# Taking attention pieces a margin later in PE's planned order, a larger gate share, and merge loads behind the sums

## The chip, the cores and the metric

The kernel runs on one core of one Trainium2 chip, in one launch. The metric is the device time of that core in microseconds; lower is better. All data are 32-bit floats. TensorE is PE in what follows, VectorE is DVE, ScalarE is ACT, GpSimd is POOL, and SP is the queue from which most DMAs are issued.

## What is computed

A backbone of two layers over 512 latent tokens and 256 context tokens of width 1024. Each layer normalises its rows, runs four kinds of attention (A, B, C, D, each with four heads of 64), merges them through sigmoid gates, and ends in a mixture of 32 experts. What the change touches is the attention and the merge:

```python
def merge_branches(h, outs, w_gate, b_gate, w_branch, w_out):
    y = None
    for n in range(N_BRANCH):                       # four branches
        t = jax.nn.sigmoid(h @ w_gate[n] + b_gate[n]) * (outs[n] @ w_branch[n])
        y = t if y is None else y + t
    return y @ w_out

for l in range(DEPTH):                              # DEPTH = 2
    h, hc = modulate(x, ...), modulate(ctx, ...)    # [512, 1024], [256, 1024]
    y, yc = token_mixer(h, hc, ..., with_ctx=l < DEPTH - 1)   # w_in, attention A B C D, merge_branches
    x = x + gt1 * y                                 # and ctx likewise in layer 0
    x = x + gt2 * hier_moe(modulate(x, ...), ...)   # top-1 group, top-2 expert in it
```

Layer 0 runs over all 768 tokens, layer 1 over the 512 latent ones (its context only serves as keys). `h @ w_gate[n]` and `outs[n] @ w_branch[n]` are the two products whose order the change moves.

## The kernel before, in words

**Products.** A product of two float matrices is made of three matmuls: each operand is split into a rounded high part and the rest (names end in H and L), and high x high, high x low and low x high are summed in PSUM (line 251). Weights come from DRAM as `wraw`, ACT makes wH (L275), DVE or, where it is told so, POOL makes wL (L276).

**Order on PE.** `dense` runs norm, attention, gates and merge of a layer with PE's order written by a planner, class `Flow`. It holds items (a piece of work with those it depends on, a latency after them, slots of SBUF that it takes, and resources that it needs: "S" for one of two score buffers in PSUM called `sps`, "bk" for one of four PSUM banks called `bk`, "P" for one of three buffers of probabilities) and a clock of its own, made of assumed durations (the tables LT). `run` goes round: the **fill**, which is `gates()`, is taken when it can go and when its work so far is below `ratio` times the work of everything else (FILL: 0.8 in layer 0, 0.4 in layer 1); otherwise `pick` takes the first item of a window of 80 that is ready and whose resources are free by the planner's clock; if there is none, the fill again. The orders of DVE, ACT, POOL and SP are made afterwards by the scheduler of the language, from the same program; each of these queues runs its instructions in that fixed order.

**Attention.** For a pair of query blocks `scores` puts q x k into an `sps` (`sps<-sk,sq`, `sps<-sc,sq`), DVE takes a minimum (L1132), ACT the exponential into `P` (L1152), DVE scales it (L1157), PE transposes `P` in groups of three 128 x 128 blocks into a `bk` (`bk<-ident,P`, L256), ACT copies each group into `pt` (L1169), and `values` multiplies with V (`bk<-pt,V`); the result goes to DRAM (`o`). Projections of later halves stand between these pieces.

**Gates.** Thirty-two units a layer, unit (n, m) for branch n and 128 output columns m, n in ORDER = (1, 0, 2, 3): 24 matmuls 128x512 (`bk<-hT,wH`, `bk<-hT,wL`; in layer 0 also 24 of 128x256 for the context), tanh on ACT (L1199), and a store to DRAM (`thd<-th`). In layer 0 ten segments of the modulation weights (`mod_seg`) are part of the fill; a step of one has to wait for the DMA of the step before.

**Merge.** `load(n)` brings back the attention's results of branch n (`orw`, in layer 0 also `orc`), splits them into oHL and ocHL, and loads and splits the weights w_br (two `wraw`). `unit(n, m)` then loads the gate from DRAM into `thm`, a buffer of the same three as `P`, makes 6 matmuls 128x512 (`sps<-oHL,wH`, `sps<-oHL,wL`; in layer 0 another 6 of 128x256), multiplies gate and product on DVE (L1253 for the first n, L1249 for the others) and adds into the sums `yl` on DVE and `yc` on POOL (L1255). For the last n the finished sums are split into yH and yL. A unit depends on `ys` (the item that allocates the sums, which itself depends on the end of the whole attention), on its load and on its gate. `w_out(0)` loads four tiles of the output weights; POOL makes their wL.

Of the kernel before, what the change touches and what calls it, by code (L numbers as in the profile page):

```python
# [142 lines left out]
class Flow:  # L143
# [13 lines left out]
    def use(self, cls, after):  # L157
        self.used.append((cls, after))

    def can(self, need):  # L160
        for c in need:
            if c == "norms" and not all(it.done for it in self.norms):
                return False
            if c in self.busy and min(self.busy[c]) > self.clk:
                return False
            if c == "pt2" and self.left["pt1"] < 2 or c == "pt1" and self.left["pt1"] < 1:
                return False
            if c in ("P", "dup") and self.left[c] < 1:
                return False
        return True  # L170
# [13 lines left out]
        self.used = []  # L184
        return self.clk - t0

    def pick(self, todo):
        blocked, soon = False, []
        for it in todo[:WINDOW]:
            if it.on:  # L190
                ready = it.ready
            else:
                if any(not d.done for d in it.deps):
                    continue
                ready = max([d.t + it.lat for d in it.deps], default=0.0)
                if it.slots and (blocked or it.slots > self.free):
                    blocked = True
                    continue
            if ready > self.clk:
                soon.append(ready)  # L200
            elif self.can(it.need):
                return it, soon
        return None, soon

    def run(self, first=()):

        todo = [it for it in self.items if not it.done]
        while todo:
            if first and all(it.done for it in first):
                return  # L210
            f = self.fill
            ok = f is not None and not f.done and f.ready <= self.clk and all(d.done for d in f.deps) and self.can(f.need)
            if ok and self.filled < self.ratio * self.main:
                self.filled += self.step(f)
                continue
            it, soon = self.pick(todo)
            if it is not None:
                self.main += self.step(it)
                if it.done:
                    todo.remove(it)  # L220
                continue
            if ok:
                self.filled += self.step(f)
                continue
            if f is not None and not f.done:
                soon.append(f.ready)
            soon += [t for b in self.busy.values() for t in b]
            soon = [t for t in soon if t > self.clk]
            assert soon, "nothing can go on"
            self.clk = min(soon)  # L230


class Build:
# [971 lines left out]
    def merge(self):  # L1205
        nc, l, f = self.nc, self.l, self.fl
# [64 lines left out]
        ys = f.item(self.nop(0, sums), deps=self.ends, slots=4 + 2 * self.wc)  # L1271
# [2 lines left out]
        self.ysplit, self.wo = ([], []), {}  # L1274
        for n in ORDER:
            if n == ORDER[-1]:
                f.items.append(f.item(self.nop(0, lambda: self.w_out(0)), deps=self.ends[-1:], slots=9))
            e = {1: 1, 0: 3, 2: 5, 3: 7}[n]
            ld = f.item(self.nop(0, lambda n=n: load(n)), deps=[self.ends[e], self.gate[8 * n]], lat=0.0, slots=k)
            us = [f.item(unit(n, m), deps=[ys, ld, self.gate[8 * n + m]], lat=self.LT["th"], need=("S",)) for m in range(8)]  # L1280
            f.items += [ld] + us + [f.item(self.nop(6 + self.wc), deps=us)]

# [699 lines left out]
NT2 = 3  # L1982
GE = False
UPOOL = (3,)
FILL = (0.8, 0.4)
WINDOW = 80
ORDER = (1, 0, 2, 3)
PEX = 2
# [27 lines left out]
```

## Time and profile before

| | us |
|---|---|
| median of 3 runs | 2233.44 (2230.81 to 2235.84) |
| the profiled execution: its own time | 2233.74 |
| its span in the trace | 2232.0 |
| layer 0: attention's first and last matmul | 45.5, 713.6 |
| layer 0: first and last merge matmul | 723.0, 839.5 |
| layer 0: first expert matmul | 971.1 |
| layer 1: first transpose of h, last attention matmul | 1297.4, 1771.4 |
| layer 1: first and last merge matmul | 1777.3, 1870.0 |
| layer 1: first expert matmul, end | 1956.1, 2232.0 |

The lower rows are starts in the trace, from the start of the span. A "tail" is the stretch from the attention's last matmul to the merge's last: 713 to 841 and 1771 to 1870. In each stretch PE's busy time against the length says how much PE stood idle; the waits say for whom. Durations of matmuls are read from the distance between the starts of neighbours in a row, since the printed length of one includes its way through the pipeline.

### The profile page before, as it was taken

The numbers are of one execution on the slowest core, as the hardware profiler recorded it, in microseconds if no ns is written. First come the engines' busy times: TensorE is split into PE (matmuls) and PEld (weight loads), VectorE is DVE, ScalarE is ACT, GpSimd is POOL, SyncE is SP. The second block draws the span as 40 slices with busy tenths as digits, with TensorE's granted clock in tenths as the row PEclk, the third lists the DMA queues.
The fourth block names the chain that finished last, engine by engine and source line by source line (L and its number), as shares of the span: only waits on it lengthen the run. The fifth ranks groups of instructions, "written<-read, shape, count | busy, mean of one in ns | idle before, by whom it ended". The sixth has DMA issues, their size and how long they took to land. (4 is left out here: it accounts for less than half of the span.)

```text
span 2232.0 us, 34108 instructions
## 1 busy us (share of the span) xinstructions
PE 2068.5 (93%) x13005; PEld 1524.7 (68%) x13005; DVE 1288.5 (58%) x2655; ACT 808.8 (36%) x1817; POOL 295.7 (13%) x321
## 2 busy tenths in 40 slices
PE   5999999999999988969999979999999998699997
PEld 3878777777887877934444468877888787644443
DVE  4464454345544565677777766555466476746655
ACT  4454454344444221212222235565455432211112
POOL 1101100011100144230000031000020013200000
PEclk8999999999999998979999989999999999899999
DMA  7452443543223555679999423112212387699992
GB/s 280 144 195 95 152 155 113 171 149 119 81 78 115 188 187 197 227 254 402 365 366 364 178 76 107 55 48 90 90 46 86 121 259 263 226 379 407 406 406 80
DMA packets 141813, 430.92 MB, mean 193 GB/s; under 512 B 19344, under 2 KB 32032, under 8 KB 141648
## 3 DMA queue, kind: packets, MB, share of 16 engines
q1 hardware_dynamic: 127120, 388.36, 48.4%
q0 software_dynamic: 13088, 35.10, 4.8%
q10 hardware_dynamic: 1440, 5.24, 0.6%
q8 instruction: 104, 1.70, 0.3%
q14 instruction: 61, 0.50, 0.1%
HBM read 398.67 MB, written 36.78 MB: 195 GB/s over the span
## 5 line engine op out<-in xcount | busy, mean ns | idle before, releaser
L251 PE MATMUL bk<-hT,wH 128*128 128x512 f32 (+1 forms) x1760 | 480.2, 360 | 2.8 <-ACT wH L275 2.1
L251 PEld LDWEIGHTS bk<-hT,wH 128*128 128x128 f32 x1760 | 300.1, 189 | 51.4 <-issue 8.1
L251 PE MATMUL bk<-hT,wL 128*128 128x512 f32 (+1 forms) x880 | 311.8, 354 | 7.6 <-DVE wL L276 7.6
L1786 DVE TENSOR_TENSOR x<-x,sps 128x1024 f32<-128x1024 f32 x166 | 195.5, 1216 | 101.0 <-PE sps L1785 100.6
L1727 PE MATMUL bk<-e,xT 128*64 128x512 f32 x1056 | 245.8, 603 | 0.0
L251 PE MATMUL bk<-wH,hT 128*128 128x256 f32 x1248 | 240.5, 287 | 1.3 <-DVE sk L276 1.0
L251 PEld LDWEIGHTS bk<-wH,hT 128*128 128x128 f32 x1248 | 200.0, 193 | 5.3 <-DVE sk L276 1.3
L251 PEld LDWEIGHTS bk<-hT,wL 128*128 128x128 f32 x880 | 166.3, 189 | 33.4 <-DVE wL L276 9.8
L275 ACT ACTIVATE wH<-wraw 128x1024 fp32r<-128x1024 f32 x132 | 139.1, 1058 | 125.1 <-DMA wraw<-in_w_gate_dram 41.5
L276 DVE TENSOR_TENSOR wL<-wraw,wH 128x1024 fp32r<-128x1024 f32 x112 | 138.8, 1245 | 70.2 <-ACT wH L275 39.4
L251 PE MATMUL bk<-wL,hT 128*128 128x256 f32 x624 | 177.2, 284 | 0.0
L1727 PEld LDWEIGHTS bk<-e,xT 128*64 128x64 f32 x1056 | 72.1, 138 | 142.9 <-issue 125.7
L1152 ACT ACTIVATE P<-sps,m 128x768 f32<-128x768 f32 (+2 forms) x160 | 126.5, 792 | 77.0 <-DVE m L1132 52.7
L1169 ACT ACTIVATE pt<-bk 128x384 f32<-128x384 f32 (+1 forms) x288 | 120.8, 467 | 74.7 <-PE bk L256 73.6
L1785 PE MATMUL sps<-yeH,to 128*128 128x512 f32 x332 | 142.7, 430 | 2.4 <-ACT yeH L275 1.4
L256 PE MATMUL bk<-ident,P 128*128 128x128 f32 x800 | 121.2, 282 | 19.2 <-ACT pt L1169 7.3
L1785 PE MATMUL sps<-yeL,to 128*128 128x512 f32 x332 | 132.2, 398 | 1.7 <-DVE yeL L276 1.7
L322 POOL TENSOR_TENSOR rr<-rs,mhalf 128x1 f32<-128x1 f32 (+1 forms) x72 | 52.3, 727 | 572.5 <-DVE rs L318 500.9
L1750 PE MATMUL bk<-e,gT 128*64 128x512 f32 x528 | 122.3, 606 | 1.5 <-ACT gT L1743 1.5
L256 PEld LDWEIGHTS bk<-ident,P 128*128 128x128 f32 x800 | 91.7, 142 | 46.7 <-ACT pt L1169 15.4
L251 PEld LDWEIGHTS bk<-wL,hT 128*128 128x128 f32 x624 | 120.3, 193 | 0.6
L1733 ACT ACTIVATE eth<-bk 128x256 f32<-128x256 f32 x33 | 12.7, 385 | 285.7 <-PE bk L1727 285.7
(355 smaller groups left out, 3671.4 us busy)
## 6 DMA issues: line engine op xcount, KB each, us to landing
e<-in_w_dram SPq DMA_DIRECT2D x384, 512.0 KB, 7.5
wmod<-in_w_mod_dram SPq DMA_DIRECT2D x96, 512.0 KB, 4.6
wraw<-in_w_gate_dram SPq DMA_DIRECT2D x64, 512.0 KB, 4.0
wraw<-in_w_in_dram SPq DMA_DIRECT2D x36, 512.0 KB, 4.9
thd<-th SPq DMA_DIRECT2D x64, 256.0 KB, 3.4
thm<-thd SPq DMA_DIRECT2D x32, 384.0 KB, 3.1
wraw<-in_w_br_dram SPq DMA_DIRECT2D x16, 512.0 KB, 4.0
wraw<-in_w_out_dram SPq DMA_DIRECT2D x16, 512.0 KB, 6.1
```

The source lines that it names most:

```text
L251: return self.nc.tensor.matmul(out, lhsT, rhs, **kw)
L256: return self.nc.tensor.transpose(out, src, self.ident if ident is None else ident)
L275: nc.scalar.activation(H, src, AF.Copy)
L276: (eng or nc.vector).tensor_tensor(L, src, H.bitcast(F32), op=ALU.subtract)
L322: self.nc.gpsimd.tensor_tensor(r[:, :n], o[:, :n], self.mhalf.to_broadcast([128, n]), op=ALU.pow)
L1152: nc.scalar.activation(Pt[:, :n], S[:, lo:768], AF.Exp, scale=-1.0, bias=m, accum_out=sm)
L1169: nc.scalar.activation(PT[gi][:, :w, qi * 128:(qi + 1) * 128], v, AF.Copy)
L1727: nc.tensor.matmul(box["h"][64 * z:64 * z + 64, :], xT(k, z), W(z, k // 2)[:, (k % 2) * 512:(k % 2 + 1) * 512], start=k == 0, stop=k == 7, ...
L1733: nc.scalar.activation(th[s], H[s, :256], AF.Tanh, scale=0.5)
L1750: nc.tensor.matmul(Y[n][64 * z:64 * z + 64, :], gT[:, k, 64 * z:64 * z + 64], W(z, 4 + k)[:, n * 512:(n + 1) * 512], start=k == 0, stop=k ...
L1785: nc.tensor.matmul(ps[:, c], to[s, t * 128:(t + 1) * 128], w[s, c], start=i == 0, stop=i == 1)
L1786: nc.vector.tensor_tensor(self.x1[t] if out is None else out, self.x1[t], ps, op=ALU.add)
```

## The change

`can` and `pick` get a margin: while the fill could go (`ok`), an item counts as ready, and a PSUM buffer as free, only when it has been so for MARGIN = 1000 units of the planner's clock. When the fill can't go, the margin is 0. The ratio of the fill goes from (0.8, 0.4) to (0.85, 0.45). In `merge()`, `w_out(0)` and `load(n)` of all branches but the first wait for `ys`, so that the sums get their slots first, and the first load may start only if slots for itself and for the sums are left. PE's instructions are the same in number and kind.

```diff
-    def can(self, need):
+    def can(self, need, margin=0.0):
...
-            if c in self.busy and min(self.busy[c]) > self.clk:
+            if c in self.busy and min(self.busy[c]) + margin > self.clk:
                 return False
...
-    def pick(self, todo):
+    def pick(self, todo, margin):
...
-            if ready > self.clk:
+            if ready + margin > self.clk:
                 soon.append(ready)
-            elif self.can(it.need):
+            elif self.can(it.need, margin):
                 return it, soon
...
-            it, soon = self.pick(todo)
+            it, soon = self.pick(todo, MARGIN if ok else 0.0)
...
             if n == ORDER[-1]:
-                f.items.append(f.item(self.nop(0, lambda: self.w_out(0)), deps=self.ends[-1:], slots=9))
+                f.items.append(f.item(self.nop(0, lambda: self.w_out(0)), deps=[ys], slots=9))
             e = {1: 1, 0: 3, 2: 5, 3: 7}[n]
-            ld = f.item(self.nop(0, lambda n=n: load(n)), deps=[self.ends[e], self.gate[8 * n]], lat=0.0, slots=k)
+            early = n == ORDER[0]
+            ld = f.item(self.nop(0, lambda n=n: load(n)), deps=[self.ends[e], self.gate[8 * n]] + ([] if early else [ys]),
+                        lat=0.0, slots=k + early * ys.slots)
...
-FILL = (0.8, 0.4)
+FILL = (0.85, 0.45)
+MARGIN = 1000.0
```

What that does to the order is seen at three places. The first is PE near the end of layer 1's attention (branch D). `ident,P` are the transposes of probabilities, `sk,sq` and `sc,sq` scores, `pt,V` values, `hT,wH` and `hT,wL` gates. Before:

```order
L251 MATMUL bk<-hT,wL 128x512
L256 MATMUL bk<-ident,P 128x128 x12
L251 MATMUL sps<-sk,sq 128x512 x2
L251 MATMUL sps<-sc,sq 128x256 x2
L251 MATMUL sps<-sk,sq 128x512 x2
L251 MATMUL sps<-sc,sq 128x256 x2
L251 MATMUL bk<-hT,wH 128x512 x2
L251 MATMUL bk<-hT,wL 128x512
L251 MATMUL bk<-pt,V 64x256 x12
```

and now:

```order
L251 MATMUL bk<-pt,V 64x256 x12
L256 MATMUL bk<-ident,P 128x128 x3
L251 MATMUL sps<-sk,sq 128x512 x2
L251 MATMUL sps<-sc,sq 128x256 x2
L251 MATMUL bk<-hT,wH 128x512 x2
L251 MATMUL bk<-hT,wL 128x512
L256 MATMUL bk<-ident,P 128x128 x6
L251 MATMUL sps<-sk,sq 128x512 x2
L251 MATMUL sps<-sc,sq 128x256 x2
L251 MATMUL bk<-hT,wH 128x512 x2
L251 MATMUL bk<-hT,wL 128x512
L256 MATMUL bk<-ident,P 128x128 x3
```

Twelve transposes, four PSUM banks' worth, stood in one piece; now the groups stand apart, with gates and scores between them.

The second place is DVE at the first merge load of layer 0, `load(1)`: oHL and ocHL are its splits, of `orw` and `orc`, and the wL with neighbours wraw, wH are splits of weights, in both orders of a gate and of w_br. The L1132, L1156 and L1157 rows belong to scores. Before:

```order
L276 TENSOR_TENSOR oHL_7406<-orw_7402,oHL_7405 128x1024
L1132 TENSOR_REDUCE m_7444<-sps_7439 128x1
L1132 TENSOR_REDUCE m_7457<-sps_7452 128x1
L1156 RECIPROCAL rc_7449<-sum_7447 128x1
L1157 TENSOR_SCALAR P_7446<-P_7446,rc_7449 128x768
L276 TENSOR_TENSOR ocHL_7412<-orc_7409,ocHL_7412 128x512
L276 TENSOR_TENSOR wL_7418<-wraw_7415,wH_7417 128x1024
L1156 RECIPROCAL rc_7462<-sum_7460 128x1
L276 TENSOR_TENSOR wL_7502<-wraw_7499,wH_7501 128x1024
```

and now:

```order
L919 TENSOR_TENSOR dup_7458<-xnh_7449,g3_5853 128x3x64
L276 TENSOR_TENSOR oHL_8084<-orw_8080,oHL_8083 128x1024
L276 TENSOR_TENSOR wL_7601<-wraw_7598,wH_7600 128x1024
L276 TENSOR_TENSOR ocHL_8090<-orc_8087,ocHL_8090 128x512
L1101 COPY oT_7515<-bk_7510 128x256
L706 SCALAR_TENSOR_TENSOR sc_6698<-bk_7518,sc_6698 64x2x128
L276 TENSOR_TENSOR sc_6698<-bk_7518,sc_6698 128x128
L1132 TENSOR_REDUCE m_7549<-sps_7544 128x1
```

The gate's wL (7502 before, 7601 now) stood behind oHL, ocHL and a wL of w_br; now it stands behind oHL alone.

The third place is DVE in layer 1's merge. L1253 (first branch) and L1249 are the products of gate and merge, one for each unit; the wL between are splits of gate weights (18481, 18559) and of w_br. Before:

```order
L1253 SCALAR_TENSOR_TENSOR yl_18292<-thm_18434,sps_18436 128x512
L276 TENSOR_TENSOR wL_18481<-wraw_18478,wH_18480 128x1024
L276 TENSOR_TENSOR oHL_18448<-orw_18444,oHL_18447 128x1024
L276 TENSOR_TENSOR wL_18454<-wraw_18451,wH_18453 128x1024
L276 TENSOR_TENSOR wL_18460<-wraw_18457,wH_18459 128x1024
L276 TENSOR_TENSOR wL_18559<-wraw_18556,wH_18558 128x1024
L1249 SCALAR_TENSOR_TENSOR thm_18497<-thm_18497,sps_18499 128x512
L1249 SCALAR_TENSOR_TENSOR thm_18508<-thm_18508,sps_18510 128x512
L1255 TENSOR_TENSOR yl_18289<-yl_18289,thm_18497 128x512
L1255 TENSOR_TENSOR yl_18289<-yl_18289,thm_18508 128x512
```

and now:

```order
L1253 SCALAR_TENSOR_TENSOR yl_18567<-thm_18681,sps_18683 128x512
L1253 SCALAR_TENSOR_TENSOR yl_18567<-thm_18691,sps_18693 128x512
L1249 SCALAR_TENSOR_TENSOR thm_18725<-thm_18725,sps_18727 128x512
L1255 TENSOR_TENSOR yl_18564<-yl_18564,thm_18725 128x512
L1249 SCALAR_TENSOR_TENSOR thm_18736<-thm_18736,sps_18738 128x512
L1255 TENSOR_TENSOR yl_18564<-yl_18564,thm_18736 128x512
L1249 SCALAR_TENSOR_TENSOR thm_18747<-thm_18747,sps_18749 128x512
```

Gates and loads stood between the units of the first branch and of the second; now the gates and the first three loads are over before the first unit, and 24 units, those of three branches, follow one another with only the fourth load near their end. In numbers, from PE's order: behind the attention's last `pt,V` there stood 111 gate matmuls 128x512 and 120 of 128x256 in layer 0 and 207 of 128x512 in layer 1; now 33, 48 and 24. Of the 32 merge units 22 stood ahead of the last gate in layer 0 and 24 in layer 1; now 2 and none.

## Rows read from the trace of the kernel before

**Rows 1.** Stretches: length, then busy (count) of PE, PEld, DVE, ACT, POOL; PEclk; DMA
```profile
46.00:713.00 667.00, 644.02 (x4639) 529.33 (x4640) 323.83 (x822) 316.81 (x783) 57.68 (x89) 0.99 0.38 128
713.00:841.00 128.00, 116.22 (x635) 99.09 (x633) 73.75 (x85) 27.96 (x36) 38.28 (x30) 0.95 0.58 188
1297.00:1771.00 474.00, 450.17 (x2949) 383.28 (x2951) 275.77 (x667) 251.04 (x613) 48.70 (x50) 0.98 0.23 73
1771.00:1870.00 99.00, 94.29 (x412) 76.84 (x409) 60.21 (x74) 28.19 (x33) 17.97 (x16) 0.98 0.74 236
```

**Rows 2.** PE's waits in layer 0's attention: total us, times, longest
```profile
PE bk L251 <- DVE wL L276: 5.6, 2, 5.0
PE bk L256 <- DVE P L1157: 3.7, 3, 2.7
PE bk L256 <- ACT pt L1169: 2.8, 8, 1.1
```

**Rows 3.** Timeline at the longest of these: start, us, engine, line, [idle before <-releaser]
```profile
667.25 1.23 DVE L276 TENSOR_TENSOR oHL<-orw,oHL 128x1024 fp32r<-128x1024 f32 x1 [4.36 <-ACT oHL L275]
668.63 0.28 PE L251 MATMUL bk<-hT,wL 128*128 128x256 f32 x1
668.75 0.63 PE L251 MATMUL bk<-hT,wH 128*128 128x512 f32 x2
674.34 0.79 PE L251 MATMUL bk<-hT,wL 128*128 128x512 f32 x1 [4.95 <-DVE wL L276]
```

**Rows 4.** The stretch right behind that wait, columns as in the first group
```profile
674.00:678.00 4.00, 3.66 (x14) 3.38 (x15) 2.90 (x4) 1.37 (x4) 0.00 (x0) 0.50 0.61 219
```

**Rows 5.** PE's waits in layer 1's attention, the longest at its start and the commonest
```profile
PE sps L256 <- POOL h L620: 7.0, 2, 5.0
PE sps L256 <- DVE rs L318: 4.7, 1, 4.7
PE bk L256 <- ACT pt L1169: 4.5, 8, 1.1
```

**Rows 6.** PE's waits in layer 0's tail
```profile
PE sps L251 <- ACT wH L275: 6.1, 2, 5.5
PE sps L251 <- DVE wL L276: 3.1, 4, 1.4
```

**Rows 7.** Groups by line in layer 0's tail (723 to 841): count, busy, mean ns, idle before
```profile
L1255 POOL TENSOR_TENSOR yc<-yc,thm 128x256 f32<-128x256 f32 x23 | 27.6, 1204 | 95.0 <-DVE thm L1249 94.8
L276 POOL TENSOR_TENSOR wL<-wraw,wH 128x1024 fp32r<-128x1024 f32 x4 | 9.6, 2397 | 7.1 <-PE sps L251 4.4 <-ACT wH L275 2.7
```

**Rows 8.** Timeline of PE from the end of layer 1's attention to its merges
```profile
1771.70 0.72 PE L251 MATMUL bk<-hT,wH 128*128 128x512 f32 x2
1777.29 0.62 PE L251 MATMUL sps<-oHL,wH 128*128 128x512 f32 x2
1777.97 0.62 PE L251 MATMUL sps<-oHL,wH 128*128 128x512 f32 x2
```

**Rows 9.** Splits on DVE in layer 1's tail, by line
```profile
L276 DVE TENSOR_TENSOR wL<-wraw,wH 128x1024 fp32r<-128x1024 f32 x13 | 15.8, 1220 | 12.2 <-ACT wH L275 7.3 <-PE bk L251 4.9
```

**Rows 10.** DMA loads of thm in 713 to 841, 1771 to 1850, 1850 to 1872: KB, median to landing
```profile
thm<-thd SPq DMA_DIRECT2D x29, 384.0 KB, 3.1
...
thm<-thd SPq DMA_DIRECT2D x24, 256.0 KB, 3.9
...
thm<-thd SPq DMA_DIRECT2D x5, 256.0 KB, 6.5
```

**Rows 11.** Timeline of DVE in layer 1's last branch, where no gates are left
```profile
1854.59 0.69 DVE L1249 SCALAR_TENSOR_TENSOR thm<-thm,sps 128x512 f32<-128x512 f32 x1 [1.50 <-PE sps L251]
1859.27 0.68 DVE L276 TENSOR_TENSOR yL<-yl,yH 128x512 fp32r<-128x512 f32 x1
1863.69 0.69 DVE L1249 SCALAR_TENSOR_TENSOR thm<-thm,sps 128x512 f32<-128x512 f32 x1 [3.74 <-DMA thm<-thd]
1871.67 0.68 DVE L1255 TENSOR_TENSOR yl<-yl,thm 128x512 f32<-128x512 f32 x1
```

## The prediction

> **What bounds the kernel now.** I read the busy time by stretch first: PE holds both stretches of attention and both tails. In layer 0's attention it is busy for 644.0 of 667 us, in layer 1's for 450.2 of 474, in the tails for 116.2 of 128 and 94.3 of 99 [rows 1]. So 23.0, 23.8, 11.8 and 4.7 us of idle PE are all there is to win in the part that the change orders, and it brings no matmul more or less. Outside it (norms, routing, experts) no order moves; I price that at nothing.
>
> Then PE's waits. In layer 0's attention the longest is one for a weight split on DVE (5.0 us); the commonest are for `pt` on ACT, which has to empty a PSUM bank before the next transposes may write it (8 waits, 2.8 us), and for P on DVE (3.7 us) [rows 2]. In layer 1, 11.7 of the 23.8 us are the two waits at the start, for norms, which nothing here moves; the `pt` waits are 4.5 us [rows 5], and the rest is spread over waits of 0.2 to 1.7 us. In the tails PE waits for the splits of a load [rows 6] and, where no gates are left between the merges, for the gate that comes back by DMA as thm [rows 11].
>
> **Prices.** One matmul 128x512 takes 0.227 us (three between the starts 1777.29 and 1777.97 [rows 8]), one of 128x256 0.12 us (668.63 to 668.75 [rows 3]). A gate in layer 1 is then 24 x 0.227 = 5.4 us, a merge unit 6 x 0.227 = 1.36 us.
>
> **Part 1, the margin and the share, in the attention.** By the order 78 gate matmuls 128x512 and 72 of 128x256 move ahead of the end of layer 0's attention (17.7 + 8.6 = 26.3 us) and 183 of 128x512 in layer 1 (41.5 us). This is work that leaves the tail for the attention; by itself it costs nothing. What it can save is idle time.
>
> Layer 1: twelve transposes in a row fill four banks and wait for ACT; the order now puts other work between the groups. I take the 4.5 us of `pt` waits down to about 0.5, and of the other 7.6 us (23.8 - 11.7 - 4.5) two thirds, 5: together **-9**. The ends: only the `pt` waits go and half of them come back elsewhere, -3; all 12.1 go, -12.
>
> Layer 0: the same for `pt` is -2.3. The long wait at 674.34 [rows 3] costs 5.0 us and then about 3 more: PE runs at 0.50 of its clock, the 1.2 GHz level, in the next 4 us [rows 4]. It comes from the first merge load: its split of `orw` stands on DVE ahead of a gate's weight split. The order now puts that gate's split behind one row of the load instead of three, but still behind `orw`, which has to come by DMA. I take half, -4. Against it: where the fill waits for its own weights (the modulation segments) the margin is 0, and by the order five transposes of context pieces now stand only 1.2 to 1.9 us of matmuls behind their scores, where one did before; that one cost 2.7 us [rows 2]. Longer distances than that one's, so +2 for all. Sum with a point for small waits: **-5**. Ends: -14 (the load's wait and the clock go whole, the context pieces wait for nothing, and half of the rest of the 23.0 goes too), +3 (the load stalls as before, the context pieces take 5).
>
> **Part 2, layer 1's tail.** Before, 24 of 32 units stood among gates. While PE made a gate (5.4 us), DVE multiplied, added and split, and the next thm came in. Now 24 gate matmuls (5.4 us) remain, and then 32 units follow each other with nothing between. Who is slowest there? PE needs 1.36 us a unit. DVE needs 0.69 + 0.68 = 1.37, and with the last branch's split of the sums 2.05 [rows 11]. The DMA has three buffers: a thm lands 3.9 us after its issue [rows 10], is held for 0.69 by the product and 0.68 by the add, so three units take at least 3.9 + 1.37 = 5.3 us, 1.76 a unit; 1.53 for the first branch, which has no separate add. Before, in the one place without gates, the last branch's eight units took from 1854.59 to 1872.35 on DVE, 2.2 us each, with 3.74 us of waiting for thm [rows 11], though one of its loads was slow because other loads ran (6.5 us [rows 10]). Step by step: 5.4 for the last gates, about 2 until the first unit has its thm, 8 x 1.53 = 12.2, 16 x 1.76 = 28.2, 8 x 2.2 = 17.6, and about 3 for the loads' splits (three loads of three rows of 1.22 us [rows 9], mostly inside DVE's waits): 68.4 us. Had the stretch stayed as tight as before, it would take 99 - 41.5 = 57.5. The difference is 10.9; the last branch stays the tight one and its waits let the clock fall (not priced before), so I take **+12**. Lower end: thm lands in 3.1 us, as the larger one did in layer 0 [rows 10], now that gate weights don't share the DMA; then the middle branches go at 1.49, the first at PE's 1.36, and the tail takes 58 to 60 us: +2. Upper end: landing at 5.0, between 3.9 and 6.5: +20.
>
> DVE alone gives a floor of the same size: it is busy 60.2 us in that tail [rows 1], of which seven of the thirteen weight splits, those of gates (8.5 us [rows 9]), leave, so 52 us remain to be done behind a start of some 5 us.
>
> The Trainium skill (Perfetto Trace Analysis, section Identifying Performance Opportunities, Optimization Strategy) says that where the most-contended engine changes from one regime to the next, interleaving the regimes can help; this change takes gates and merges, which were interleaved, apart. By that rule alone the tail loses; the rows before agree as far as they go (3.74 us of waiting where no gates were left).
>
> **Part 3, layer 0's tail.** A unit is 6 x 0.227 + 6 x 0.12 = 2.1 us on PE, more than thm needs with 3.1 us, so PE stays the bound between loads. The 26.3 us that moved leave 128 - 26.3 = 101.7 if the 11.8 idle us stay. `load(3)` still stands directly ahead of its units, so its wait of 5.5 us and the splits behind it stay, somewhat shorter [rows 6]; -2. `load(0)` now stands between the second and the third unit of the first branch; its splits stand on DVE among their products, and on its DMA, late in SP's queue behind thm and the stores of gates, the products wait: at worst like load(3), 5.5 + 0.6; I take +3. POOL has four splits of 2.40 us for `w_out` in its queue among adds of 1.20 us [rows 7], and a buffer of thm is held until POOL has added; against 2.1 us a unit POOL has 0.9 to spare, so 9.6 us of splits push back some units: +3. Together **+4**. Ends: -4 (the waits for load(0)'s splits vanish and POOL's are hidden), +10.
>
> `w_out(0)` and the later loads behind the sums only change who gets slots first; in the order they stand ahead of their first users as before. Nothing.
>
> **The sum.** -9 - 5 + 12 + 4 = +2 against 2233.74 of the profiled execution, which is 0.3 above the median of 2233.44. I predict 2236. A difference of 0.2%, 4.5 us, is about what a measurement of this kernel can tell from no change.
>
> **Rivals.**
>
> 1. *The attention's waits go, and the tails stay on PE.* The margin removes the wait at 674.34 with its clock, -12 for layer 0, -11 for layer 1; thm lands in 3.1 us and the tail of layer 1 pays +3, that of layer 0 nothing: -20, 2214; with half of the load's wait left, 2220. For it: PE is busy for 95% or more of both attentions [rows 1] and the waits named are those that a margin treats. Against it: DVE's 52 us of work in layer 1's tail don't move.
> 2. *The merge becomes bound by the return of the gates.* Place: layer 1's 32 units. With a landing of 5.0 us (from about 4.2 this decides) the tail costs +20, with POOL's splits and both loads in layer 0 +9; the attention gives -5 and -9: +15, 2249. For it: the 3.74 us and the 6.5 us landing. Against it: gate weights and stores no longer use the DMA there.
> 3. *The margin doesn't do what it says in layer 0.* It holds only while the fill can go, and there the fill often waits; what is planned on assumed times is not what the trace has. Layer 0 +2, layer 1 -4, tails +4 and +12: +14, 2248.
>
> **How the numbers follow.** The forecast has 0.40 (its own range 2228 to 2244; of it 0.27 within 0.2%, 0.06 faster, 0.07 slower), rival 1 0.27 (0.26 faster, 0.01 same), rival 2 0.25 (0.23 slower, 0.02 same), rival 3 0.08 (0.06 slower, 0.01 same, 0.01 faster). That makes 0.33 faster, 0.31 same, 0.36 slower. The range for 8 in 10 goes from 2217, most of rival 1, to 2251, most of rivals 2 and 3.
>
> **What would show it.** In the profile after: PE's waits for `pt` in both attentions under 1 us in sum; the wait for wL at the first load halved or gone; attention's idle PE down to about 18 and 15 us. The attention of layer 1 ends some 32 us later behind its start, that of layer 0 some 21. In layer 1's tail PE waits for thm or the product (L1249) in every third unit, and the tail takes 68 to 70 us; if it takes under 60, part 2 is wrong and rival 1 holds. In layer 0's tail the waits stand at load(0) and load(3). I would be wrong altogether if a queue that no row here shows, SP's above all, holds a late DMA ahead of gate weights in the middle of the attention.

## The result

The changed kernel takes 2257.47 us (median of 4 runs, 2249.93 to 2263.42) against 2232.12 before (4 runs beside it): a ratio of 1.0107, 95% interval 1.0076 to 1.0138, so 17 to 31 us slower. The forecast was 2236 with a range to 2251: wrong in size and out of its range. The profiled execution took 2257.18 us with a span of 2255.4, 23.4 more than before's span. Where they went, by the same marks as in the table of before (starts in the trace); "moved" is the gates' work that the order carried from the tail into the attention, at 0.227 and 0.12 us a matmul:

| stretch | before | after | change | moved | change without it | forecast |
|---|---|---|---|---|---|---|
| layer 0, attention (first to last matmul) | 668.0 | 695.5 | +27.5 | +26.3 | +1.2 | -5 |
| layer 0, tail (to the last merge) | 125.9 | 108.7 | -17.2 | -26.3 | +9.1 | +4 |
| layer 1, attention (first h to last values) | 474.0 | 514.4 | +40.4 | +41.5 | -1.1 | -9 |
| layer 1, tail | 98.6 | 75.5 | -23.1 | -41.5 | +18.4 | +12 |
| all else | 865.5 | 861.3 | -4.2 | | -4.2 | 0 |

(Columns of stretches add up to the span within 0.1.) The tails paid as forecast in kind, and more. The attention did not give what was to pay for them. First the busy times of the changed kernel in its two attentions and two tails, to be read against [rows 1]; stretch, length, then busy time (and count) of PE, PEld, DVE, ACT, POOL, then PEclk and the DMA's share:

```profile
46.00:742.00 696.00, 670.09 (x4796) 551.95 (x4796) 329.18 (x825) 324.57 (x793) 53.34 (x89) 0.98 0.38 128
742.00:852.00 110.00, 90.57 (x477) 76.99 (x477) 68.99 (x82) 21.61 (x27) 37.69 (x30) 0.91 0.59 188
1304.00:1819.00 515.00, 492.54 (x3136) 421.52 (x3136) 285.46 (x677) 266.58 (x630) 47.31 (x50) 0.98 0.25 82
1819.00:1896.00 77.00, 59.02 (x234) 44.41 (x230) 52.47 (x66) 14.06 (x17) 16.79 (x16) 0.91 0.69 213
```

Idle PE is 25.9, 19.4, 22.5 and 18.0 us, where it was 23.0, 11.8, 23.8 and 4.7: no less in the attentions, 21 us more in the tails, and the granted clock in the tails fell from 0.95 and 0.98 to 0.91.

PE's waits in layer 0's attention (total us, times, longest), against [rows 2]:

```profile
PE bk L251 <- DMA wmod<-in_w_mod_dram: 8.4, 5, 4.4
PE bk L251 <- DVE kl L276: 3.1, 2, 2.6
...
PE bk L256 <- DVE P L1157: 1.8, 1, 1.8
PE bk L251 <- DVE wL L276: 1.7, 2, 1.2
...
PE bk L256 <- ACT pt L1169: 1.0, 3, 0.4
```

The three waits that [rows 2] lists did shrink: wL 5.6 to 1.7, P 3.7 to 1.8, pt 2.8 to 1.0, together 7.6 us. In their place stands a wait that [rows 2] doesn't have, for the weights of the modulation segments. In layer 1's attention, against [rows 5]:

```profile
PE sps L256 <- POOL h L620: 5.8, 2, 3.9
PE sps L256 <- DVE rs L318: 4.7, 1, 4.7
PE bk L256 <- ACT pt L1169: 4.2, 7, 1.7
PE bk L251 <- DVE qr L706: 2.9, 1, 2.9
```

The waits for pt, which were to fall from 4.5 to about 0.5 us, stand at 4.2.

In the tails, layer 0 (two rows, against [rows 6]) and layer 1 (the longest):

```profile
PE sps L251 <- ACT wH L275: 8.6, 1, 8.6
PE sps L251 <- DVE yc L1253: 6.3, 1, 6.3
```

```profile
PE sps L251 <- DVE thm L1249: 15.6, 8, 6.2
```

Layer 1's tail in detail. The timeline of DVE (start, us, [idle before <-releaser]) shows two things that hold the units up, the add and the return of the gate:

```profile
1841.68 0.69 DVE L1249 SCALAR_TENSOR_TENSOR thm<-thm,sps 128x512 f32<-128x512 f32 x1 [0.49 <-DMA thm<-thd]
1842.40 2.64 DVE L1255 TENSOR_TENSOR yl<-yl,thm 128x512 f32<-128x512 f32 x1
...
1847.00 2.24 DVE L1255 TENSOR_TENSOR yl<-yl,thm 128x512 f32<-128x512 f32 x1
...
1855.31 2.63 DVE L1255 TENSOR_TENSOR yl<-yl,thm 128x512 f32<-128x512 f32 x1
...
1859.89 2.88 DVE L1255 TENSOR_TENSOR yl<-yl,thm 128x512 f32<-128x512 f32 x1
...
1867.86 0.69 DVE L1249 SCALAR_TENSOR_TENSOR thm<-thm,sps 128x512 f32<-128x512 f32 x1 [2.44 <-DMA thm<-thd]
...
1875.69 0.69 DVE L1249 SCALAR_TENSOR_TENSOR thm<-thm,sps 128x512 f32<-128x512 f32 x1 [6.42 <-DMA thm<-thd]
```

and the same stretch on POOL, where the four weight splits of `w_out(0)` stand at the four long adds, and large loads at the long wait for thm:

```profile
1842.11 2.39 POOL L276 TENSOR_TENSOR wL<-wraw,wH 128x1024 fp32r<-128x1024 f32 x1 [13.79 <-ACT wH L275]
1846.29 2.40 POOL L276 TENSOR_TENSOR wL<-wraw,wH 128x1024 fp32r<-128x1024 f32 x1 [1.80 <-ACT wH L275]
1855.01 2.38 POOL L276 TENSOR_TENSOR wL<-wraw,wH 128x1024 fp32r<-128x1024 f32 x1 [6.32 <-ACT wH L275]
1859.84 2.38 POOL L276 TENSOR_TENSOR wL<-wraw,wH 128x1024 fp32r<-128x1024 f32 x1 [2.46 <-ACT wH L275]
1862.17 0.56 POOL L1289 DMA_DIRECT2D gt<-modd  x1
```

Each add is 1.6 to 2.2 us longer than its 0.69 elsewhere, 7.6 us in sum. Before has four such adds in this tail too, between 1820 and 1838 and among its gates; they take 1.36 to 2.17 us, 4.6 more than four short ones. The Trainium skill (SBUF — State Buffer, section SBUF: two separate sides) says that DVE and GpSimd share one pair of ports, that a DVE instruction with two SBUF inputs and a GpSimd instruction that reads SBUF lock it for their whole length, and that the other waits; the rows agree, each of the four adds begins within a split and ends some 0.55 us after it (the first 1842.40 + 2.64 against 1842.11 + 2.39).

### The profile page after: what moved, and what is told of

The parts are those of the page before. It is cut to its first block, busy times and chain, and to the rows that moved or that the text cites. A ratio compares the mean times of both kernels' runs of the same rounds, so it can differ in the third digit from the quotient of the medians.

```text
span 2255.4 us, 34100 instructions
## 1 busy us (share of the span) xinstructions
PE 2070.2 (92%) x13005; PEld 1528.1 (68%) x13005; DVE 1288.8 (57%) x2655; ACT 810.1 (36%) x1817; POOL 288.1 (13%) x321
## 5 line engine op out<-in xcount | busy, mean ns | idle before, releaser
L251 PE MATMUL bk<-hT,wH 128*128 128x512 f32 (+1 forms) x1760 | 486.9, 364 | 5.2 <-ACT wH L275 4.6
L251 PE MATMUL bk<-wH,hT 128*128 128x256 f32 x1248 | 245.8, 291 | 1.5 <-ACT pt L1169 0.8
L1169 ACT ACTIVATE pt<-bk 128x384 f32<-128x384 f32 (+1 forms) x288 | 126.6, 465 | 109.1 <-PE bk L256 107.7
L251 PE MATMUL sps<-oHL,wH 128*128 128x512 f32 x256 | 88.3, 428 | 36.2 <-DVE thm L1249 18.8
```

Of the source, the lines that this page charges most:

```text
L251: return self.nc.tensor.matmul(out, lhsT, rhs, **kw)
L1169: nc.scalar.activation(PT[gi][:, :w, qi * 128:(qi + 1) * 128], v, AF.Copy)
```

## The experiments

The parts of the change were first run apart, then in each layer apart; the theories were told before each run. Times of a run are set against before's runs on the same chip. Two figures are used throughout: layer 0 from attention's first matmul to the last merge (794.0 before, 804.2 after), and layer 1 from the first h to the last merge (572.6 and 589.9). Kernels that share layer 0's order in PE repeat the first within 6 us (804.2, 807.6, 802.0 with share 0.85; 784.5, 783.7, 781.7 with 0.8). Layer 1 repeats less well: with the same order on PE and three buffers for thm it takes 579.7, 588.9 and 589.9 with share 0.45, and 576.7 to 583.5 in five kernels with 0.4, most of the difference in the tail (69.6 to 76.3 and 68.6 to 76.4). Each such figure is of one profiled execution, so differences of a few us between two of them prove nothing.

**The loads alone** (margin and shares as before):

```diff
-                f.items.append(f.item(self.nop(0, lambda: self.w_out(0)), deps=self.ends[-1:], slots=9))
+                f.items.append(f.item(self.nop(0, lambda: self.w_out(0)), deps=[ys], slots=9))
...
-            ld = f.item(..., deps=[self.ends[e], self.gate[8 * n]], lat=0.0, slots=k)
+            ld = f.item(..., deps=[self.ends[e], self.gate[8 * n]] + ([] if early else [ys]), lat=0.0,
+                        slots=k + early * ys.slots)
```

> The kernel before with the third part alone: w_out(0) and the loads of all branches but the first wait for the sums; no margin, shares 0.8 and 0.4. By the order none of the 32 merge units of layer 0 now stands ahead of the last gate (22 before), in layer 1 24 as before. Theory 'bunching' (merge units in a row wait for their gates by DMA and for the splits of loads, wherever they stand): layer 0's tail +6 to +10 us, layer 1's tail unchanged, total +5 to +10. Rival 'the attention' (the slowdown comes from pieces and gates inside the attention): no change, within 4 us. Rival 'slots' (the later loads cost by themselves): both tails longer, +15 or more.

Measured: 2229.94 against 2232.92, ratio 0.9994 (0.9974 to 1.0013); 793.2 and 574.1. No change, as the rival 'the attention' has it. Layer 0's attention is 6.2 shorter and its tail 5.5 longer, near the theory's 6 to 10: with `load(1)` later, the wait for its splits at 674 is gone from the attention (waits for wL 0.7 in place of 5.6), and the tail, where all units now stand behind the gates, takes back as much.

**The shares alone** (loads and margin as before):

```diff
-FILL = (0.8, 0.4)
+FILL = (0.85, 0.45)
```

> The kernel before with the shares 0.85 and 0.45 alone. By the order 26 us of gates are left behind layer 0's attention (40 before) and 31 us behind layer 1's (47); 14 and 20 units stand among them (22 and 24 before). Bunching: a few units more in a row, +2 to +6 us, all of it in the tails. Attention: more gates in it ask for their weights sooner, so the gain of the tails is lost by waits for weight DMAs in the attention: +8 or more, tails no longer than before by their own work.

Measured: 2263.85, ratio 1.0118 (1.0089 to 1.0147). The two numbers alone cost 20 to 33 us, as much as the whole change. Without the work moved (13.5 and 15.7 us) layer 0's attention is 10.6 longer, layer 1's 17.1, the tails -3.4 and +7.7. The theory of bunching falls; the loss is in the attention. It has a name there in both layers. In layer 0 it is the wait for modulation weights, which before doesn't have; in layer 1 the wait for PSUM banks that [rows 5] has with 4.5:

```profile
PE bk L251 <- DMA wmod<-in_w_mod_dram: 7.8, 4, 3.4
```

```profile
PE bk L256 <- ACT pt L1169: 12.9, 14, 3.1
```

**No margin** (shares and loads as changed):

```diff
-MARGIN = 1000.0
+MARGIN = 0.0
```

> The changed kernel with MARGIN 0 (shares 0.85 and 0.45 and the loads behind the sums stay). Layer 0: 26 us of gates behind the attention and no unit among them; layer 1: 31 us and 20 units. Bunching: layer 0's tail +6 to +10, layer 1's +2 to +4, total +8 to +13, so the margin is what costs the rest of the 24 us. Attention: if the margin saves nothing and costs nothing, this is as slow as the changed kernel, +20 or more.

Measured: 2270.13, ratio 1.0168 (1.0132 to 1.0203); 804.4 and 596.5. Slower than the changed kernel: the margin doesn't cost, it saves some 13 us of what the shares cost. In the traces that is layer 1's attention (+15.1 without the work moved, against -1.1 with the margin), less 9.6 which layer 1's tail gives back (+8.8 against +18.4); layer 0 takes the same with and without it. The waits for pt in layer 1's attention without the margin, 4.2 with it:

```profile
PE bk L256 <- ACT pt L1169: 12.7, 15, 2.3
```

**Margin and loads, shares as before:**

```diff
-FILL = (0.85, 0.45)
+FILL = (0.8, 0.4)
```

> The changed kernel with the shares 0.8 and 0.4 of before (margin and loads behind the sums stay). By the order the margin alone already draws the gates into the attention: 29 us are left behind layer 0's, 5 us behind layer 1's, with 8 and 0 units among them. Bunching: layer 1's tail is as tight as in the changed kernel, +15 to +20 against before, layer 0's +4 to +8; total +15 to +25. Rival 'the share is what costs' : the margin's savings in the attention show, -5 to -10 there, and the total is within 8 us of before.

Measured: 2231.70, ratio 0.9991 (0.9976 to 1.0007); 784.5 and 576.7. Without the larger shares the change does in total what the forecast said of the whole, nothing. Without the work moved, layer 0's attention is at -12.7, its tail +3.3, layer 1's attention -7.4, its tail +11.5, in sum -5.3 in these four (forecast +2, by -5, +4, -9, +12); the profiled execution, 2225.59, lies 6 us under the median, so the sum agrees better than these four show. Since the loads alone are at 0.9994, no gain of the margin is shown at these shares: what the attentions give, the tails take. The rival named in the expectation holds: the share is what costs.

**The share of one layer at a time** (margin and loads kept):

```diff
-FILL = (0.85, 0.45)
+FILL = (0.85, 0.4)    # share0;  share1: (0.8, 0.45)
```

> The changed kernel with layer 1's share back at 0.4 (margin, loads behind the sums and layer 0's 0.85 stay). Theory 'share in layer 0': the larger share of layer 0 makes gates and modulation steps ask for their weights faster than the DMA brings them; layer 0 up to its last merge takes 800 to 806 us against 784.5 with 0.8 and 794.0 before, and the total is +12 to +20 against before. Rival 'share in layer 1': this kernel is within 5 us of before, and share 0.45 in layer 1 carries the loss.

> The changed kernel with layer 0's share back at 0.8 (margin, loads behind the sums and layer 1's 0.45 stay). Share in layer 0: total +4 to +12 against before, from layer 1 alone, where attention and merge take 584 to 592 us (576.7 with share 0.4, 572.6 before). Rival 'share in layer 1': +18 or more.

Measured: layer 0's share alone 2248.32 against 2232.49, ratio 1.0062 (1.0041 to 1.0084), 807.6 in layer 0. Layer 1's alone 2236.21, ratio 1.0016 (1.0003 to 1.0028), 588.9 in layer 1. Most of the loss is layer 0's. Layer 1's 0.45 costs some 6 us in its attention: 514.4, 512.7, 510.1 and 514.9 in four kernels with it, 506.2 to 508.1 in nine with 0.4.

**The planned latency of a modulation step.** In layer 0's attention the changed kernel has a hole, PE busy for 4.5 of 12 us while the DMA engines are at 0.99:

```profile
424.00:436.00 12.00, 4.50 (x43) 1.44 (x43) 2.87 (x3) 2.75 (x4) 0.00 (x0) 0.75 0.99 364
436.00:446.00 10.00, 7.92 (x47) 6.82 (x48) 3.92 (x4) 3.39 (x5) 2.01 (x4) 0.78 0.25 79
```

SP's queue just ahead of it: loads of a projection unit (in_w_in) stand between the loads of a modulation segment, 512 KB each:

```profile
422.24 0.42 SPq L285 DMA_DIRECT2D wraw<-in_w_in_dram  x1
422.76 0.92 SPq L403 DMA_DIRECT2D wmod<-in_w_mod_dram  x2
427.29 0.33 SPq L1102 DMA_DIRECT2D o<-oT  x1
427.66 0.42 SPq L285 DMA_DIRECT2D wraw<-in_w_in_dram  x1
428.18 0.86 SPq L403 DMA_DIRECT2D wmod<-in_w_mod_dram  x2
```

and what PE waited for in the hole:

```profile
434.77 1.08 PE L251 MATMUL bk<-wmod,silu 128*32 128x256 f32 x8 [4.44 <-DMA wmod<-in_w_mod_dram]
```

```diff
-          ... th=8000.0, mod=1500.0,
+          ... th=8000.0, mod=2500.0,
```

> The changed kernel with the planned latency of a modulation step in layer 0 at 2500 in place of 1500, so that PE's order leaves more work between two of them. Theory 'modulation weights': PE's waits for wmod in layer 0's attention (8.4 us, the longest 4.4) fall below 4 us, the hole around 424 to 436 us of the changed kernel, with PE busy for 4.5 of 12 us, goes, and layer 0 up to its last merge is 6 to 14 us shorter than the changed kernel's 804.2. Rival 'not the modulation' (the lost time of layer 0 lies in many small waits): within 4 us of the changed kernel there.

Measured: 2238.27 against 2232.49, ratio 1.0028 (1.0013 to 1.0044): 18 to 19 us under the changed kernel, from one planned number. Layer 0 takes 791.2, its waits for wmod are no more among PE's, PE is busy for 11.1 of the 12 us. The edit takes 13.0 us off layer 0, the hole and the smaller waits for wmod together. The trace is 24 us shorter in all; 10 of these are in layer 1, whose order on PE is the same (589.9 and 579.7, the spread told above).

**Six buffers for thm**, first with margin, loads and the shares of before, later in the changed kernel and in the kernel before:

```diff
-            th = self.sm.tile([128, NTOK], F32, name="thm", tag="P", bufs=NP)
+            th = self.sm.tile([128, 3, 256], F32, name="thm", tag="pt", bufs=NPT).rearrange("p a b -> p (a b)")
```

> Margin and loads behind the sums with the shares 0.8 and 0.4, and thm in the six buffers of pt, which are free by then, in place of the three of P. Theory 'three buffers' (the gates' return by DMA paces the units in a row): layer 1's tail falls from 68.6 to 58 to 62 us, PE's waits for the product from 10.2 us to under 4; layer 0's tail -1 to -4; total 6 to 12 us under before. Rival 'DVE' (the adds, stretched to 2 or 2.5 us while POOL splits weights, pace them): the tail stays within 3 us of 68.6 and the total is within 4 us of before.

> The changed kernel with thm in the six buffers of pt in place of the three of P. Theory 'three buffers': the tail of layer 1 falls from 75.5 to 60 to 65 us, PE's waits for the product there from 15.6 us to about 5, while layer 0's attention keeps its hole at the modulation weights; total 8 to 16 us under the changed kernel, so still 8 to 16 over before. Rival 'modulation alone': less than 5 us under the changed kernel.

> The kernel before with thm in the six buffers of pt. Theory 'three buffers cost where units stand in a row': there are only 8 such units in layer 1, so -2 to -5 us, all in layer 1's last branch. Rival 'the buffers help everywhere': -8 or more, and then the margin gives nothing in the kernel with both.

Measured: with margin and loads 2219.26, ratio 0.9947 (0.9932 to 0.9962), layer 1's tail 62.3 in place of 68.6; in the changed kernel 2244.45 against 2233.73, ratio 1.0055 (1.0033 to 1.0077), tail 61.3 in place of 75.5; in the kernel before 2225.22, ratio 0.9951 (0.9934 to 0.9968), tail 92.7 in place of 98.6. PE's wait for the product in the changed kernel's tail with six buffers, 15.6 with three:

```profile
PE sps L251 <- DVE thm L1249: 5.0, 4, 1.6
```

Three buffers did pace the units in a row: 14 of the tail's 18.4 us go with them, and the four kernels with the units in a row, six buffers and `w_out(0)` as in the diff take 61.3 to 62.4 us there, against 68.6 to 76.4 with three. But before gains more from them than I gave it (9 us by the medians, 11 by the ratio, 5.9 of it in layer 1's tail): the rival 'the buffers help everywhere' is right. Like against like, with six buffers on both sides, taking gates and merges apart still costs layer 1's tail some 10 us (61.3 against 92.7 less the 41.5 moved). The version with margin, loads, shares 0.8 and 0.4 and six buffers has the best median here, 8 to 15 us under before; but before with six buffers alone is at 0.9951, so with six buffers no gain of the margin is shown.

**The splits of w_out(0) on DVE**, in the last version:

```diff
-            self.wo[i] = self.unit(..., 8, None, self.nc.gpsimd)
+            self.wo[i] = self.unit(..., 8, None, self.nc.gpsimd if half else None)
```

> Margin, loads behind the sums, shares 0.8 and 0.4, thm in six buffers, and the four splits of w_out(0) on DVE in place of POOL in both layers. Theory 'POOL stretches DVE's adds' (four adds of 2.2 to 2.6 us in place of 0.69 stand where POOL splits): all adds of layer 1's tail take 0.69 us; DVE takes four splits of 1.22 instead, 4.9 against 7.2 us: layer 1's tail -1 to -3 us, layer 0's -2 to +2. Rival: the adds are long for another reason and stay so; then the tail is 4 to 5 us longer.

Measured: 2225.78, ratio 0.9960 (0.9945 to 0.9975); layer 1's tail 69.9, 7.6 longer. The adds in layer 1's tail, first with the splits on POOL, then on DVE (line, count, busy, mean ns):

```profile
L1255 DVE TENSOR_TENSOR yl<-yl,thm 128x512 f32<-128x512 f32 x24 | 23.6, 989 | 0.6
```

```profile
L1255 DVE TENSOR_TENSOR yl<-yl,thm 128x512 f32<-128x512 f32 x24 | 16.0, 686 | 0.1
```

The cause of the long adds is shown: without splits on POOL every add takes 0.69 us. The price was wrong, and not by the splits alone. On DVE they take 4.9 us and wait 4.4 for their weights, with the units' products behind them. But DVE also waits 8.2 us for thm, all of it ahead of the first split, where the kernel with the splits on POOL has no such wait:

```profile
1816.08 0.69 DVE L1249 SCALAR_TENSOR_TENSOR thm<-thm,sps 128x512 f32<-128x512 f32 x1 [4.33 <-DMA thm<-thd]
```

POOL's queue shows what changed. Its loads for the next stage, four of them of 512 KB, stood behind the four splits, 43 us into the tail; without the splits they are issued 8 us into it. First the first of these loads with the splits on POOL and on DVE, then the loads of thm from 8 to 30 us into the tail, in the same order (KB, median us to landing):

```profile
1831.83 0.56 POOL L1289 DMA_DIRECT2D gt<-modd  x1
```

```profile
1799.27 0.53 POOL L1289 DMA_DIRECT2D gt<-modd  x1
```

```profile
thm<-thd SPq DMA_DIRECT2D x13, 256.0 KB, 3.9
```

```profile
thm<-thd SPq DMA_DIRECT2D x9, 256.0 KB, 9.9
```

So this run doesn't price the long adds: it took them away and brought other loads against the return of the gates. POOL was the better place here, where the splits also held those loads back.

**The amount, or the place?** The shares could cost because more gates want weights in the same time, or because a segment of modulation weights falls on other loads. The same edit of the latency in the fast version:

> Margin, loads behind the sums, shares 0.8 and 0.4, thm in six buffers, and the planned latency of a modulation step at 2500. Theory 'modulation weights': the wait of 2.5 us for wmod and the 2 us of slow clock behind it go from layer 0's attention, -2 to -7 us against the same kernel with 1500 (2219 us). Rival: what is left of waits for wmod is too little, within 2 us.

Measured: 2237.44 against 2233.73, ratio 1.0014 (1.0001 to 1.0026): 15 to 18 us slower than with 1500, where I expected a gain. Layer 0's attention has no wait for wmod any more, but another one instead:

```profile
PE bk L256 <- DVE P L1157: 10.5, 9, 3.2
```

My reading is that these transposes of P are taken too early, as in the wait of 2.7 us of [rows 2], since with a longer planned latency the fill can go less often, and while it can't, the margin is 0. That is not shown: the same latency at share 0.85 leaves 3.3 us of these waits. Four more runs, two with other shares in layer 0 (0.825 and 0.9, layer 1 at 0.4), two with the segments put one gate earlier:

```diff
-            if segs and i % 2 == 1:
+            if segs and i % 2 == 0:
```

> Margin and loads behind the sums, thm in three buffers, layer 1's share 0.4, layer 0's 0.825. By the order 24 us of gates are left behind layer 0's attention (29 with 0.8, 13 with 0.85). Theory 'amount' (each step of the share costs, since more gates want their weights in the same time): layer 0 up to its last merge takes 790 to 798 us, between 784.5 with 0.8 and 807.6 with 0.85. Theory 'coincidence' (what costs is where a modulation segment falls against loads of projection weights and against pieces that are then taken without margin): it can lie outside these two, and its waits are at other places than 424 to 436 us.

> As s825 with 0.9 in layer 0: no gate is left behind the attention. Amount: 815 us or more up to layer 0's last merge, waits for modulation weights above 9 us. Coincidence: 790 to 812, with waits for modulation weights that may be smaller than the 9.1 us of share 0.85.

> Margin, loads behind the sums, shares 0.85 and 0.4, thm in three buffers; the ten segments of modulation weights are put ahead of the even gates in place of the odd ones, one gate earlier. The same work, share and loads. Amount: 804 to 810 us up to layer 0's last merge, as with the odd ones (807.6). Coincidence: off by 6 us or more, with the hole at 424 to 436 gone or elsewhere.

> Margin, loads behind the sums, shares 0.8 and 0.4, thm in six buffers, the segments ahead of the even gates. Amount: as with the odd gates, 2219 us, within 3 us. Coincidence: layer 0's attention differs by 5 us or more in either direction, with its waits for modulation weights or for P.

Measured, with what went before, layer 0 from attention to last merge, all with the margin:

| share in layer 0 | segments, latency | layer 0, us | whole kernel: ratio to before |
|---|---|---|---|
| 0.8 | odd, 1500 | 784.5 | 0.9991 |
| 0.825 | odd, 1500 | 796.3 | 1.0048 (1.0032 to 1.0063) |
| 0.85 | odd, 1500 | 807.6 | 1.0062 (1.0041 to 1.0084) |
| 0.9 | odd, 1500 | 784.6 | 0.9972 (0.9953 to 0.9991) |
| 0.85 | even, 1500 | 790.8 | 1.0010 (0.9990 to 1.0031) |
| 0.85 | odd, 2500 (share 0.45) | 791.2 | 1.0028 |
| 0.8, six buffers | odd, 1500 | 781.7 | 0.9947 |
| 0.8, six buffers | even, 1500 | 799.1 | 0.9992 (0.9977 to 1.0007) |
| 0.8, six buffers | odd, 2500 | 799.5 | 1.0014 |

The largest share, with no gate left for the tail, is as fast in layer 0 as the smallest. One gate's shift of the segments takes 17 us off at 0.85 and adds 17 at 0.8 (12 and 10 by the ratios of the whole kernel). So the place decides and not the amount. Of the expectations, 0.825 alone would fit the amount, 0.9 lies under the ranges of both theories, and the two shifts are as 'coincidence' said, except that at 0.8 the longest wait in the hole is for ACT's part of a weight split, whose weights came late from DRAM (3.9 us), and only then for wmod (1.7). The stretch 424 to 436 us in the kernel with 0.9, where the changed one has its hole:

```profile
424.00:436.00 12.00, 12.00 (x91) 8.80 (x92) 9.10 (x14) 6.43 (x12) 2.01 (x4) 1.00 0.48 173
```

and with 0.8, six buffers and even segments:

```profile
424.00:436.00 12.00, 6.37 (x56) 2.47 (x55) 4.15 (x7) 4.45 (x8) 2.01 (x4) 0.85 0.84 286
```

The traces also tell how much is waiting and how much is clock. Layer 0's attention at share 0.85, with odd and then with even segments, has the same 4795 matmuls:

```profile
45.50:744.50 699.00, 672.89 (x4795) 554.88 (x4795) 329.31 (x825) 324.77 (x793) 54.43 (x89) 0.98 0.37 128
```

```profile
45.50:729.70 684.20, 665.60 (x4795) 548.55 (x4796) 329.63 (x829) 323.00 (x793) 54.43 (x89) 0.99 0.38 131
```

PE is idle for 26.1 and 18.6 us, 7.5 apart, and busy for 7.3 longer with the same work at the lower granted clock: half and half.

## Why the prediction was wrong, point by point

**The step that failed** is in part 1. The sum has no term for the larger share: "This is work that leaves the tail for the attention; by itself it costs nothing. What it can save is idle time." I took the margin and the share as one part, priced the margin's savings and let the share only move matmuls. The runs take them apart. The two shares cost 20 to 33 us by themselves and some 26 us on top of margin and loads (2257.47 against 2231.70); without them the total doesn't change. Layer 0's attention, forecast at -5, came out at +1.2 with the share and at -12.7 without it; layer 1's, forecast at -9, at -1.1 and -7.4. Moving the work is indeed not what costs: at 0.9 all of it moves and layer 0 is as fast as at 0.8. A new pace of the fill shifts everything else against it, and at 0.85 a modulation segment falls on the loads of a projection unit: 8.4 us of waiting for wmod where there was none, with a lower clock behind it. My last sentence came near, "SP's above all, holds a late DMA ahead of gate weights in the middle of the attention", but as an afterthought, with no price and no chance, and of other weights.

Of the 21 us between forecast and trace (+23.4 against +2) 14 are in the attentions and 11.5 in the tails, less 4.2 in the rest.

**The waits of the attention.** In layer 0 the waits for pt, P and the load's split shrank by 7.6 us. "The load's wait half gone" was too careful: its 5.0 us are gone, and the margin isn't needed for that, since they are gone with the loads alone and with the shares alone too. In layer 1 the first term failed: of 4.5 us of waits for pt 4 were to go, and 4.2 are left (3.4 with share 0.4). The margin works on them all the same, on those that the larger share brings: 12.7 without it. Without the shares both attentions gave 20 us, where I had 14; the agreement with the forecast is one of the sum more than of its terms.

**Layer 1's tail.** Forecast +12, range +2 to +20; measured +18.4, and +11.5 to +19.3 in the seven other kernels with the margin and three buffers, all with the same gates left, so +12 lies within what these kernels do. The mechanism, thm's three buffers, was right: six give 14 us back in the changed kernel. The sum has no term for the long adds beside POOL's splits, 7.6 us of DVE's time here and 4.6 before; what they cost the tail no run shows. Its lower end, 58 to 60 us, leaves out the 3 us for the loads' splits.

**Layer 0's tail.** Forecast +4, up to +10; measured +9.1. The term for load(0) (+3) measured 6.3: its ocHL waits for `orc`, which SP issued only at 761. Load(3) was to be 2 shorter than 5.5 and took 8.6, for the same reason:

```profile
820.86 1.90 SPq L1241 DMA_DIRECT2D thm<-thd  x2
...
822.85 0.86 SPq L1231 DMA_DIRECT2D orc<-o  x2
...
827.45 0.63 ACT L275 ACTIVATE ocHL<-orc 128x512 fp32r<-128x512 f32 x1 [3.95 <-DMA orc<-o]
...
829.08 1.22 PE L251 MATMUL sps<-oHL,wH 128*128 128x512 f32 x2 [8.58 <-ACT wH L275]
```

The loads of orc stood in SP's queue behind loads of thm, which wait there for a free buffer: between 740 and 850 the queue waited 44.0 us, up to 9.4 at once, for DVE's adds, which free thm.

**The rivals.** Rival 2 (2249) had the tails' mechanism and most of their size, but let the attention give 14 us. Rival 3 said that the margin does little in layer 0; at share 0.85 that is so in length (804.4 without it, 804.2 with it; at 0.8 it is not, 793.2 and 784.5), but its reason, the margin of 0 while the fill can't go, is not shown: the 10.5 us of waits for P in the kernel with the latency at 2500, share 0.8 and six buffers would fit it. The interleaving rule of the Trainium skill that the prediction cites (Perfetto Trace Analysis, section Identifying Performance Opportunities, Optimization Strategy) agrees with layer 1's tail: gates and merges taken apart cost it 11.5 to 19.3 us with three buffers and some 10 with six on both sides.

**What stays open.** Why 0.45 costs 6 us in layer 1's attention with the margin: single waits of 2 to 3 us (qr, a split on POOL) are at other places, and no run takes them apart. Why layer 1's tail differs by up to 8 us between kernels with the same order on PE there was not tried either.

## What to carry to other kernels

In a planned order, two numbers that change the pace of one stream shift it against all the others: cost the loads that the shifted stream meets in the DMA queue, not only the matmuls that move, and try the numbers around the one chosen, since here 0.8, 0.85 and 0.9 in layer 0 gave -2, +14 and -6 us. Before work is taken apart that used to hide a return trip through DRAM, give that trip more buffers: buffers that another stage has left free are there for nothing, and here they alone gave 8 to 11 us. Before work is taken off a queue, ask what stands behind it and will start earlier. And change one knob of such a table at a time: the margin's part and the share's loss were in one diff, and the sum had no term for the share.

## What the runs showed of the hardware

A DVE add of two SBUF tiles, 0.69 us alone, takes longer when it begins within a split on POOL and ends 0.54 to 0.55 us after the split: 2.24 to 2.88 us in four of four meetings in layer 1's tail of the changed kernel, 1.36 to 2.17 in four of four before, 2.18 to 2.64 in four of four with margin, old shares and six buffers, and never when the splits are on DVE. In the hole of the changed kernel twelve microseconds at a DMA share of 0.99 moved 364 GB/s and left PE busy for 4.5 us of them; the granted clock was 0.75 in these and 0.78 in the ten behind them. A gate of 256 KB that SP issued at 1864.16, behind two loads for load(3) and among POOL's loads of 512 KB (from 1862.17), was there at 1875.69, 11.5 us later; the median before was 3.9 [rows 10]. With POOL's loads issued early in the tail the median of nine such loads was 9.9 us.
